# The first mixer's input products of two chunks by a seven-product scheme from the third channel block on, and scaled weights split at their first use

## The chip, the cores and the metric

One Trainium2 chip, one of its cores. The metric is the device time of one execution in microseconds (us). Before the change the median of three timed runs is 1886.26 us (1881.32, 1886.26 and 1886.28).

## What is computed

A decoder trunk of two layers over x of 1 x 2048 x 1024 float32. Layer 0 is a gated short convolution, layer 1 an attention without softmax over 8 heads of 64 whose keys and values come from one shared projection.

```
h = rmsnorm(x, norm_a);  B, C, X, G = split(h @ w_in_a, 4)        # 1024 x 4096
x = x + ((B * conv3(C * X)) * silu(G)) @ w_out_a                  # causal, width 3
k, v = split(rmsnorm(x, norm_kv) @ w_kv, 2)                       # 1024 x 1024
q, g = split(rmsnorm(x, norm_b) @ w_in_b, 2)                      # 1024 x 1024
z = (q @ k.T) / 8, strictly causal
rev = reverse cumulative sum over keys of log_sigmoid(-z)
o = exp(z + rev) @ v
x = x + (o * silu(g)) @ w_out_b
out = rmsnorm(x, norm_f)
```

## The kernel before

Everything is kept transposed (features on the partitions, positions along the free axis, in reverse order) and worked in four chunks of 512 positions, c = 0 to 3. The 1024 features are KD = 8 tiles of 128. Every operand is split into a high part (a cast on ACT, L175) and a low part (a subtraction on DVE, L176, in `split`), and a product is three matmuls per tile: hi x hi, hi x lo, lo x hi. So one gate of one channel block for one chunk (`mm3`, L209) is 8 x 3 = 24 matmuls of 128x512. A gate's raw weights (`wr_*`, 512 KB) come by a DMA that SP issues, are split into a tile `whl_*` of 1 MB, and are stored to DRAM in split form (`sw_*`); whoever needs them again loads that (`load_w`, L184 to L196). There are 4 buffers for split tiles (NWB) and 2 for raw ones (NRAW).

The program starts with `mixer_in((0, 1))`: the input products of chunks 0 and 1 together, so that a weight tile serves both. Its loop runs over the 8 channel blocks cb and in each over the two chunks, and takes the gates C, X, B, G in that order: 8 x 2 x 4 = 64 gates. Gate results lie in three pairs of PSUM banks in turn. Behind the gates ACT and DVE compute the convolution (`cv_*`, L339 and after) and the gating (`sg_*`), and SP stores `y_d[c][cb]`. The norm of chunks 0 and 1 is applied late: the products run on x times the gain, and 1/rms (`rs_c`) multiplies afterwards. While that goes on, a second stream computes the statistics of chunks 2 and 3 (`stats_x`) and runs `fold_gains` (L359 to L372): it multiplies all of w_kv and w_in_b by their norm's gain on DVE (L368), splits them and stores them in DRAM, 32 half tiles of 128x512.

After it `proj_out(0)` (`po_*`, L376) reads y back, splits it and multiplies by w_out_a; `proj_k`, `proj_q` and `proj_v` of chunk 0 follow (12 gates, with four of `proj_g` later), interleaved with `mixer_in((2,))` and the attention of chunk 0; then the other chunks in the same manner, and a tail with the output projection and the last norm.

The program is written as generators that `merge` interleaves by estimated costs. The order of the instructions on each engine is then fixed when the program is built, by a scheduler which simulates the engines. On the chip each engine takes its list in order and waits where an operand isn't ready. A DMA on SP's list that waits for something holds up every DMA behind it.

Of the kernel before, what the change touches and what calls it, by code (L numbers as in the profile page):

```python
# [8 lines left out]
F32 = mybir.dt.float32  # L9
# [5 lines left out]
P = 128  # L15
S = 2048
D = 1024
# [4 lines left out]
NR, NW, NT, NL, NWB, NRAW, NA, NWTS = 5, 8, 4, 5, 4, 2, 16, 2  # L22
# [7 lines left out]
NB = 3  # L30
GRP, GRY, SLACK = 3, 6, 8
# [14 lines left out]
def kernel(  # L46
# [117 lines left out]
    def square_into(acc, src, first, nm, eng=nc.vector, early=False):  # L164
        if first:
            nc.scalar.activation(acc, src, AF.Square)
        else:

            tag = "wth" if early else "t"
            sq = sb.tile([P, CH], F32, name=f"sq_{nm}", tag=tag, bufs=NT if tag == "t" else NWTS)  # L170
            nc.scalar.activation(sq, src, AF.Square)
            eng.tensor_add(acc, acc, sq)
# [5 lines left out]
    def w_tile(nm, kt=KD):  # L178
        return sb.tile([P, 2, kt, P], F32R, name=f"whl_{nm}", tag="whl", bufs=NWB)
# [4 lines left out]
    def load_w(src, key, nm, kt=KD, eng=nc.vector):  # L184

        if key not in split_d:
            wt = w_tile(nm, kt)
            raw = sb.tile([P, kt, P], F32, name=f"wr_{nm}", tag="wraw", bufs=NRAW)
            nc.sync.dma_start(out=raw, in_=src.rearrange("(k p) n -> p k n", p=P))
            split(wt[:, 0], wt[:, 1], raw, eng)  # L190
            split_d[key] = dram.tile([P, 2, kt, P], F32, name=f"sw_{nm}")
            nc.sync.dma_start(out=split_d[key], in_=wt.bitcast(F32))
            return wt
        wt = w_tile(nm, kt)
        nc.sync.dma_start(out=wt.bitcast(F32), in_=split_d[key])
        return wt  # L196
# [6 lines left out]
    def mm3(ps, wts, a, kt=KD):  # L203

        hi, lo = wts[:, 0], wts[:, 1]
        n = 0
        for k in range(kt):
            for w, m in ((hi, 0), (hi, 1), (lo, 0)):
                ins = nc.tensor.matmul(ps, w[:, k, :], a[k][:, m, :], start=n == 0, stop=n == 3 * kt - 1)  # L209
                if fine[1] and len(anchors) > SLACK and n % GRP == 0:  # L210

                    tc.add_manual_dep(ins.ins, anchors[-1 - SLACK].ins.name, PACE, reason="pace")
                n += 1
                if n % fine[0] == 0 and n < 3 * kt:
                    yield MM * fine[0]

    def rest(n):
        return MM * (n - (n - 1) // fine[0] * fine[0])
# [7 lines left out]
    def norm_x_late(c, between=None):  # L226

        hc, xs = [], []
        for k in range(KD):
            if k == 1 and between is not None:  # L230
                between()
            tag, bufs = (("w", NW), ("R", NR) if k < NR else ("ld", NL))[c]
            x = sb.tile([P, CH], F32, name=f"xh_{c}_{k}", tag=tag, bufs=bufs)
            nc.sync.dma_start(out=x, in_=xT[k * P:(k + 1) * P, cols(c)])
            xs.append(x)
            ga = gains["a"][:, k:k + 1]
            hk = act_tile(f"h_{c}", k)
            nc.scalar.activation(hk[:, 0, :], x, AF.Copy, scale=ga)
            nc.vector.scalar_tensor_tensor(out=hk[:, 1, :], in0=x, scalar=ga, in1=hk[:, 0, :].bitcast(F32),
                                           op0=ALU.mult, op1=ALU.subtract)  # L240
            hc.append(hk)
        return hc, xs

    def squares(c, xs):
        acc = sb.tile([P, CH], F32, name=f"acc_h{c}", tag="acc", bufs=2)
        for k, x in enumerate(xs):
            square_into(acc, x, k == 0, f"h{c}{k}", nc.gpsimd, early=True)
        return acc

    def late_rms(c, y):  # L250
        pb = bcast(y, f"h{c}")
        r = sb.tile([P, CH], F32, name=f"rs_{c}", tag="w", bufs=NW)
        nc.scalar.copy(r, pb)
        r2 = sb.tile([P, CH], F32, name=f"rs2_{c}", tag="w", bufs=NW)
        nc.scalar.activation(r2, pb, AF.Square)
        return r, r2

    rx = {}

    def stats_x(c):  # L260

        acc = sb.tile([P, CH], F32, name=f"acc_h{c}", tag="acc", bufs=2)
        for k in range(KD):
            square_into(acc, load_x(c, k, "s"), k == 0, f"h{c}{k}", early=True)
        y = const.tile([P, 4], F32, name=f"rx_{c}")
        rx[c] = rstd(acc, f"h{c}", y)
        yield 1.0
# [14 lines left out]
    late_acc, late = {}, {}  # L282

    def mixer_in(cs):
# [3 lines left out]
        for cb in range(KD):  # L288
            wts = {}
            for c in cs:  # L290
# [5 lines left out]
                def gate(g, i):  # L296
                    if c not in h:
                        if c == 0:
                            load_first = lambda: wts.update({g: load_w(w_src(i), (g, cb), f"{g}{cb}_{cs[0]}")})
                            h[c], late_acc[c] = norm_x_late(c, load_first)  # L300
                        else:
                            h[c], xs = norm_x_late(c)
                            late_acc[c] = rstd(squares(c, xs), f"h{c}")
# [43 lines left out]
                if c in late:  # L347
                    nc.vector.tensor_mul(sg, pG, late[c][0])
                    nc.scalar.activation(sg, sg, AF.Sigmoid)
                    nc.vector.tensor_mul(t, t, late[c][1])  # L350
# [3 lines left out]
                nc.vector.tensor_mul(t, t, pG)  # L354
                nc.sync.dma_start(out=y_d[c][cb], in_=t)
                yield rest(24)


    def fold_gains():  # L359

        for nm, src, gain in (("kv", w_kv, gains["kv"]), ("b", w_in_b[0], gains["b"])):
            for i in range(KD):
                split_d[nm, i] = dram.tile([P, 2, KD, P], F32, name=f"sw_{nm}{i}")
                for j in range(0, KD, 4):
                    hi, lo = (sb.tile([P, 4, P], F32R, name=f"fold{m}_{nm}{i}_{j}", tag="og", bufs=KD) for m in range(2))
                    raw = lo.bitcast(F32)
                    nc.sync.dma_start(out=raw, in_=src[j * P:(j + 4) * P, i * P:(i + 1) * P].rearrange("(k p) n -> p k n", p=P))
                    nc.vector.tensor_mul(raw, raw, gain[:, j:j + 4].unsqueeze(2).to_broadcast([P, 4, P]))  # L368
                    split(hi, lo, raw)
                    for m, t in enumerate((hi, lo)):  # L370
                        nc.sync.dma_start(out=split_d[nm, i][:, m, j:j + 4, :], in_=t.bitcast(F32))
                yield 1.0  # L372
# [3 lines left out]
    def proj_out(c):  # L376

        y = []
        for k in range(KD):
            y.append(act_tile(f"y_{c}", k))  # L380
            t = ld512(f"yr_{c}_{k}")
# [27 lines left out]
    def proj_k(c, kb):  # L409
        wts = load_w(None, ("kv", kb), f"k{c}_{kb}")  # L410
# [9 lines left out]
    def proj_q(c, qb):  # L420
        wts = load_w(None, ("b", qb), f"q{c}_{qb}")
# [7 lines left out]
    def proj_v(c, vb):  # L429
        wts = load_w(None, ("kv", 4 + vb), f"v{c}_{vb}")  # L430
# [12 lines left out]
    def proj_g(c, gb):  # L443
        wts = load_w(None, ("b", 4 + gb), f"gg{c}_{gb}")
# [175 lines left out]
    def out_b_last(c):  # L620
# [3 lines left out]
        for ob in range(KD):  # L624
# [3 lines left out]
            yield from mm3(ps, wts, og, kt=3)  # L628
# [10 lines left out]
        for ob in range(KD):  # L639
            ps = lin(f"pol_{ob}")  # L640
            yield from mm3(ps, wl[ob // 4][:, :, ob % 4:ob % 4 + 1, :], og[3:4], kt=1)
# [88 lines left out]
    run(take(m01, TA / 4))  # L730
    merge((m01, 1.75 * TA), (chain(iter((DLY,)), stats_x(2), stats_x(3), fold_gains()), 18.0 + DLY))
# [47 lines left out]
```

## Time and profile before

| | |
|---|---|
| timed runs | 1881.32 to 1886.28 us, median 1886.26 |
| profiled execution | 1879.31 us, its span 1877.6 us |
| PE, busy share of the span | 94% |
| DVE, ACT, POOL | 67%, 41%, 24% |
| mean granted PE clock | 0.979 |
| DMA | 460.44 MB, 245 GB/s |
| mixer of chunks 0 and 1 | from the start to 369.4 us, where `po` begins |

The span is that of the profiled execution between its first and last instruction; the 1.7 us outside it belong to the launch. PE is TensorE, DVE VectorE, ACT ScalarE, POOL GpSimd, SP the engine that issues most DMAs. Busy shares are means over stages with different limits, so the parts below go by stages.

### The profile page before, as it was taken

The page shows a single profiled execution, that of the slowest core. Times are in us where ns is not written, and L with a number is a line of the kernel's source. Part 1 is how long each engine was busy: PE and PEld are TensorE (multiplying, and loading weights), DVE is VectorE, ACT ScalarE, POOL GpSimd, SP SyncE. Part 2 cuts the span into 40 slices and gives each one's busy share as a digit, 9 for nine tenths or more (in the row PEclk, how much of TensorE's full clock was granted, in tenths as well). Part 3 has the DMA queues.
Part 4 walks back from the last instruction along what each step waited for, and adds up shares of the span by engine and source line. Part 5 has one row for each costly group of instructions (what it writes and reads, how often), then busy time and mean ns, then how long its engine had stood idle before and what let it go on. Part 6 is the DMA issues. An engine that isn't in the chain of part 4 may idle for free.

```text
span 1877.6 us, 24951 instructions
## 1 busy us (share of the span) xinstructions
PE 1771.9 (94%) x8312; PEld 1447.6 (77%) x8312; DVE 1261.9 (67%) x1927; ACT 772.7 (41%) x1497; POOL 450.4 (24%) x822
## 2 busy tenths in 40 slices
PE   7999999999999999999999999999988998988783
PEld 5888888888778878887888888888766886866562
DVE  7876534554243364478785478787858889889984
ACT  6423212231232143345443244454535556556642
POOL 5100000101111032132221122232223214547543
PEclk9999999999999999999999999999999999999896
DMA  9999865697978798867677766566586667778763
GB/s 292 309 324 332 307 195 165 209 328 280 336 250 281 227 330 257 290 207 250 216 253 244 248 195 204 183 215 198 180 300 196 223 194 265 260 238 278 225 196 130
DMA packets 238480, 460.44 MB, mean 245 GB/s; under 512 B 18448, under 2 KB 133136, under 8 KB 213776
## 3 DMA queue, kind: packets, MB, share of 16 engines
q1 hardware_dynamic: 178272, 400.09, 63.0%
q10 hardware_dynamic: 59920, 58.74, 10.9%
q8 instruction: 66, 1.08, 0.2%
q14 instruction: 62, 0.51, 0.1%
q0 software_dynamic: 160, 0.02, 0.1%
HBM read 322.73 MB, written 136.05 MB: 244 GB/s over the span
## 4 chain that ended last, share of the span: by engine, by line
PE 74%; DVE 10%; DMA 7%; issue 4%; ACT 2%; POOL 2%; SPq 0%; ACTq 0%; POOLq 0%; DVEq 0%
PE pX L209 9%; PE pB L209 9%; PE po L209 9%; PE pG L209 9%; PE pC L209 8%; PE wt L526 4%; PE pv L209 4%; PE pk L209 3%; PE pq L209 3%; DVE R L514 3%; PE pg L209 3%; PE av L536 3%; PE av L535 2%; PE z L500 2%; PE z L501 2%
## 5 line engine op out<-in xcount | busy, mean ns | idle before, releaser
L514 DVE TENSOR_TENSOR_SCAN R<-R,R,ones 128x512 f32<-128x512 f32 x192 | 255.0, 1330 | 25.2 <-ACT R L503 24.7
L503 ACT ACTIVATE R<-z 128x512 f32<-128x512 f32 (+1 forms) x320 | 174.0, 544 | 185.0 <-PE z L501 72.7
L176 DVE TENSOR_TENSOR wtl<-wt,wth 128x512 fp32r<-128x512 f32 (+1 forms) x320 | 186.2, 601 | 79.9 <-ACT wth L175 76.8
L175 ACT CAST wth<-wt 128x512 fp32r<-128x512 f32 (+1 forms) x320 | 159.6, 528 | 184.7 <-PE wt L526 150.3
L518 DVE TENSOR_TENSOR w<-w,R 128x512 f32<-128x512 f32 (+1 forms) x320 | 207.7, 658 | 19.6 <-POOL R L511 2.1
L209 PE MATMUL pC<-h,whl_C 128*128 128x512 f32 x768 | 189.8, 396 | 11.0 <-ACT whl_C L175 8.0
L513 POOL COPY R<-R 128x1 f32<-128x1 f32 x192 | 117.4, 613 | 340.9 <-DVE R L514 308.6
L209 PE MATMUL po<-y,whl_o 128*128 128x512 f32 x768 | 189.2, 393 | 2.4 <-DVE x L394 2.0
L209 PE MATMUL pX<-h,whl_X 128*128 128x512 f32 x768 | 186.3, 392 | 1.3 <-DVE cv L354 1.3
L209 PE MATMUL pB<-h,whl_B 128*128 128x512 f32 x768 | 185.9, 392 | 0.0
L209 PE MATMUL pG<-h,whl_G 128*128 128x512 f32 x768 | 185.7, 392 | 0.0
L526 PE MATMUL wt<-ident,w 128*128 128x128 f32 x1088 | 176.8, 278 | 7.5 <-DVE w L518 4.5
L209 PEld LDWEIGHTS pC<-h,whl_C 128*128 128x128 f32 x768 | 143.5, 189 | 44.1 <-ACT whl_C L175 8.0
L505 ACT ACTIVATE w<-z 128x512 f32<-128x512 f32 (+1 forms) x320 | 172.1, 543 | 2.5 <-PE wt L526 2.4
L209 PEld LDWEIGHTS pX<-h,whl_X 128*128 128x128 f32 x768 | 143.5, 188 | 31.5 <-DVE cv L354 1.5
L209 PEld LDWEIGHTS po<-y,whl_o 128*128 128x128 f32 x768 | 142.7, 188 | 32.1 <-DVE x L394 2.2
L209 PEld LDWEIGHTS pB<-h,whl_B 128*128 128x128 f32 x768 | 143.5, 188 | 29.7
L209 PEld LDWEIGHTS pG<-h,whl_G 128*128 128x128 f32 x768 | 143.6, 188 | 29.5
L526 PEld LDWEIGHTS wt<-ident,w 128*128 128x128 f32 x1088 | 137.4, 143 | 36.0 <-DVE w L518 6.9
L536 PE MATMUL av<-wtl,vv 128*128 128x512 f32 (+1 forms) x320 | 127.3, 401 | 27.0 <-DVE wtl L176 26.5
L514 DVE TENSOR_TENSOR_SCAN R<-R,ones 128x512 f32<-128x512 f32 (+3 forms) x128 | 116.4, 915 | 37.0 <-POOL R L509 32.8
L500 PE MATMUL z<-kt,q 128*128 128x512 f32 (+1 forms) x320 | 129.3, 406 | 5.7 <-ACT w L505 2.8
(172 smaller groups left out, 2685.1 us busy)
## 6 DMA issues: line engine op xcount, KB each, us to landing
whl_o<-sw_o SPq DMA_DIRECT2D x24, 1024.0 KB, 5.3
kt<-k_d ACTq DMA_DIRECT2D x80, 256.0 KB, 4.0
vv<-v_d ACTq DMA_DIRECT2D x80, 256.0 KB, 3.7
whl_C<-sw_C SPq DMA_DIRECT2D x16, 1024.0 KB, 5.9
whl_X<-sw_X SPq DMA_DIRECT2D x16, 1024.0 KB, 5.3
whl_B<-sw_B SPq DMA_DIRECT2D x16, 1024.0 KB, 5.8
whl_G<-sw_G SPq DMA_DIRECT2D x16, 1024.0 KB, 5.3
whl_k<-sw_kv SPq DMA_DIRECT2D x16, 1024.0 KB, 7.0
```

The lines of the kernel that those rows point to most:

```text
L175: nc.scalar.copy(hi, src)
L176: eng.tensor_sub(lo, src, hi.bitcast(F32))
L209: ins = nc.tensor.matmul(ps, w[:, k, :], a[k][:, m, :], start=n == 0, stop=n == 3 * kt - 1)
L500: nc.tensor.matmul(ps[:, lom:CH], q2[:, 0, qi * P:(qi + 1) * P], kt[:, lom:CH], start=True, stop=False)
L501: nc.tensor.matmul(ps[:, lom:CH], q2[:, 1, qi * P:(qi + 1) * P], kt[:, lom:CH], start=False, stop=True)
L503: nc.scalar.activation(R[:, lo + 1:CH + 1], ps[:, lo:CH], AF.Sigmoid, scale=-0.125)
L505: nc.scalar.activation(w[:, lo:CH], ps[:, lo:CH], AF.Sigmoid, scale=0.125)
L513: nc.gpsimd.tensor_copy(R[:, 0:1], carry[qi])
L514: nc.vector.tensor_tensor_scan(out=R[:, lo + 1:CH + 1], data0=R[:, lo + 1:CH + 1], data1=ones[:, 0:1].to_broadcast([P, CH - lo]), initial= ...
L518: nc.vector.tensor_mul(w[:, lo:CH], w[:, lo:CH], R[:, lo:CH])
L526: nc.tensor.transpose(wt[:, qi * P:(qi + 1) * P], ws[qi][:, kb * P:(kb + 1) * P], ident)
L536: ins = nc.tensor.matmul(av[:, 0:n], vs, wl[:, 0:n], start=False, stop=final)
```

## The change

Five edits go together.

1. **Seven products for eight.** `mixer_in((0, 1))` runs as before for channel blocks 0 and 1 (NPL = 2). From block 2 on `mixer_fast` takes the gates in pairs, (C, X) and (B, G): 12 units. A unit is two gates by two chunks by two halves of the features, which are eight half products of 4 x 3 = 12 matmuls. The scheme of Strassen in Winograd's form does it with seven: a11 by b11, s1 by t1, s2 by t2, s4 by b22, a12 by b21, s3 by t3, a22 by t4, where a are weight half tiles, b the halves of x in the two chunks, and s and t sums and differences of them. Three banks collect them; ACT copies four partial sums out (`keep`), DVE adds.
2. **Operands for it.** During block 1 `fast_operands` scales x of both chunks by gain and 1/rms (16 DVE operations), POOL forms 16 differences, and 28 tiles are split (a cast and a subtraction each). For each unit `fast_weights` loads four raw half tiles of 256 KB, splits eight tiles, stores four.
3. **`fold_gains` is gone.** w_kv and w_in_b are scaled and split where first used (`gain=` in `load_w`): 12 gates in the projections of chunk 0, and four in `proj_gate(2)` much later.
4. **Half tiles.** A weight tile holds 4 of the 8 feature tiles: 8 buffers of 512 KB for 4 of 1 MB, 4 raw buffers of 256 KB for 2 of 512 KB. Each weight DMA becomes two.
5. **Small ones.** The late gating uses Silu and drops a DVE product; the last block of y for chunk 0 stays on the chip; buffers move (x of chunk 1 lies in the buffers `og`, `ld`, `vv` and `ot`), and the two `merge` lines get other numbers.

```diff
-NR, NW, NT, NL, NWB, NRAW, NA, NWTS = 5, 8, 4, 5, 4, 2, 16, 2
+NR, NW, NT, NL, NWB, NRAW, NA, NWTS = 5, 8, 4, 5, 8, 4, 16, 2
+NPL = 2
+Q = 4
...
+        for j in range(0, kt, Q):
+            wt = w_tile(f"{nm}_{j}")
+            if first:
+                raw = sb.tile([P, Q, P], F32, name=f"wr_{nm}_{j}", tag="wraw", bufs=NRAW)
+                nc.sync.dma_start(out=raw, in_=src[j * P:(j + Q) * P, :].rearrange("(k p) n -> p k n", p=P))
+                if gain is not None:
+                    nc.vector.tensor_mul(raw, raw, gain[:, j:j + Q].unsqueeze(2).to_broadcast([P, Q, P]))
+                split(wt[:, 0], wt[:, 1], raw, eng)
+                nc.sync.dma_start(out=split_d[key][:, :, j:j + Q, :], in_=wt.bitcast(F32))
+            else:
+                nc.sync.dma_start(out=wt.bitcast(F32), in_=split_d[key][:, :, j:j + Q, :])
...
-        for cb in range(KD):
+        for cb in range(KD if len(cs) == 1 else NPL):
+            if cb == NPL - 1 and len(cs) > 1:
+                fast_operands()
...
-    def fold_gains():
...
+    def fast_weights(n, cb, gs):
+        if n % 2 == 0:
+            raws = [sb.tile([P, Q, P], F32, name=f"fr_{nm}_{i}", tag="wraw", bufs=NRAW) for i in range(4)]
+        else:
+            pair = sb.tile([P, 2, Q, P], F32, name=f"fr_{nm}", tag="hl", bufs=1)
+            raws = [pair[:, 0], pair[:, 1]] + [sb.tile([P, Q, P], F32, name=f"fr_{nm}_{i}", tag="ot", bufs=2) for i in range(2)]
...
+            if key == "a22":
+                nc.vector.tensor_add(a22, a21, a22)
+                sp("s1", a22)
+                nc.gpsimd.tensor_sub(a21, a11, a21)
+                nc.vector.tensor_sub(a11, a22, a11)
+                sp("s2", a11)
+        nc.gpsimd.tensor_sub(a12, a12, a11)
+        sp("s4", a12)
+        sp("s3", a21)
...
+    def mixer_fast():
+            for k in range(Q):
+                for i, m in ((0, 0), (0, 1), (1, 0)):
+                    beat[:] = [nc.tensor.matmul(bank, w[:, i, k, :], ops[b][k][m], start=start and n == 0,
...
+            yield product(a, w["a11"], "b11", True, False)
+            c0 = keep(f"f1_{nm}", a)
+            yield product(d, w["s1"], "t1", True, False)
+            p5 = keep(f"f5_{nm}", d)
+            if not final:
+                ws[n + 1] = fast_weights(n + 1, *units[n + 1])
+            if prev:
+                yield last_product(n - 1)
+            yield product(a, w["s2"], "t2", False, False)
+            c1 = keep(f"f2_{nm}", a)
+            yield product(d, w["s4"], "b22", False, True)
+            nc.vector.tensor_add(c1, c1, d)
+            if not final:
+                yield product(c, w["a12"], "b21", True, True)
+                nc.vector.tensor_add(c0, c0, c)
+            yield product(a, w["s3"], "t3", False, False)
...
-        wts = load_w(None, ("kv", kb), f"k{c}_{kb}")
+        wts = load_kv(kb, f"k{c}_{kb}")
...
-    run(take(m01, TA / 4))
-    merge((m01, 1.75 * TA), (chain(iter((DLY,)), stats_x(2), stats_x(3), fold_gains()), 18.0 + DLY))
+    run(take(m01, TA / 2))
+    merge((m01, 1.3 * TA), (chain(iter((DLY,)), stats_x(2), stats_x(3)), 2.0 + DLY))
```

How it moves the instructions shows at three places. The first is DVE at the end of channel block 1, which in the changed program comes right before the first unit with B and G (`B2`). `op_t4_2` and `op_t4_3` are operands made from x of chunk 1 (`xh_1_6`, `xh_1_7`), `cv_1_1` is the plain gating of block 1, `f1_C2` a sum of the unit before, `fr_B2_0` and `fr_B2_1` are raw weights and `whl_*_B2` their split tiles.

```order
L177 TENSOR_TENSOR op_t4_2_1_1154<-xh_1_6_555,op_t4_2_0_1153 128x512
L374 TENSOR_TENSOR cv_1_1_1059<-cv_1_1_1059,sg_1_1_1089 128x512
L177 TENSOR_TENSOR op_t4_3_1_1158<-xh_1_7_560,op_t4_3_0_1157 128x512
L560 TENSOR_TENSOR f1_C2_1218<-f1_C2_1218,fc_C2_1205 128x512
L177 TENSOR_TENSOR whl_a21_B2_1246<-fr_B2_0_1235,whl_a21_B2_1246 128x512
L177 TENSOR_TENSOR whl_a22_B2_1251<-fr_B2_1_1236,whl_a22_B2_1251 128x512
L465 TENSOR_TENSOR fr_B2_1_1236<-fr_B2_0_1235,fr_B2_1_1236 128x512
L177 TENSOR_TENSOR whl_s1_B2_1256<-fr_B2_1_1236,whl_s1_B2_1256 128x512
```

Before, the weights of a gate needed one such subtraction; now the tile s1 needs two loads, two casts, an addition, a cast and a subtraction. Counted from the first product of `fast_operands` with the 1/rms of chunk 1, the third of these rows is the 70th on DVE (14 products with a scalar, 56 additions, subtractions and products of two tiles) and the last the 75th.

The second place is SP at the same time. `fr_B2_0` and `fr_B2_1` take the two buffers `ot` in which `xh_1_6` and `xh_1_7` lie; `y_d_1_1` is the store of `cv_1_1`.

```order
L463 DMA sw_B2_1244<-whl_a11_B2_1241 256x1x512
L458 DMA fr_B2_0_1235<-in_w_in_a_dram 128x4x128
L377 DMA y_d_1_1_96<-cv_1_1_1059 128x512
L458 DMA fr_B2_1_1236<-in_w_in_a_dram 128x4x128
```

Both loads can be issued only when DVE has read `xh_1_6` and `xh_1_7` for the rows `op_t4_2` and `op_t4_3` above. On PE the first product that needs them, s1 by t1 of unit B2, stands behind seven products: a11, s1, a12, s2, s4 and s3 of unit C2 and a11 of unit B2.

The third place is SP in the projections of chunk 0. Before, the split weights of a gate came in one load each (`whl_*`, from `sw_*`):

```order
L195 DMA whl_k0_1_3913<-sw_kv1_1426 128x2048
L195 DMA whl_q0_1_3947<-sw_b1_2264 128x2048
L195 DMA whl_v0_1_3978<-sw_kv5_1834 128x2048
```

Now raw halves (`wr_*`) are loaded, and the halves split before them (`whl_*`) stored, by turns:

```order
L201 DMA sw_k0_1_4151<-whl_k0_1_0_4152 256x1x512
L197 DMA wr_v0_1_0_4244<-in_w_kv_dram 128x4x128
L201 DMA sw_k0_1_4151<-whl_k0_1_4_4159 256x1x512
L197 DMA wr_v0_1_4_4251<-in_w_kv_dram 128x4x128
L201 DMA sw_q0_1_4198<-whl_q0_1_0_4199 256x1x512
L197 DMA wr_v0_2_0_4295<-in_w_kv_dram 128x4x128
```

So a raw load stands behind a store which waits for the split of an earlier gate; before, a load waited only for a free buffer.

In the whole program PE has 144 matmuls fewer, DVE 140 operations more, ACT 153 more and POOL 40 more, and SP issues 166 DMAs more.

219 lines of the change are left out of this document (174 added, 45 removed).

## The prediction

> **What bounds the kernel now.** I read the page first: the busy shares, the slices, and the chain that ended last, by engine.
>
> ```profile
> PE 1771.9 (94%) x8312; PEld 1447.6 (77%) x8312; DVE 1261.9 (67%) x1927; ACT 772.7 (41%) x1497; POOL 450.4 (24%) x822
> PE   7999999999999999999999999999988998988783
> DVE  7876534554243364478785478787858889889984
> PE 74%; DVE 10%; DMA 7%; issue 4%; ACT 2%; POOL 2%; SPq 0%; ACTq 0%; POOLq 0%; DVEq 0%
> ```
>
> PE is busy for 94% of the span and carries 74% of the last chain. A slice is 47 us, so the mixer of chunks 0 and 1 is the first eight, and in seven of them PE shows a 9. What a change there is worth is read from that stage, so the next view is the busy time by stretches (PE, PEld, DVE, ACT, POOL busy us, granted PE clock, DMA share, GB/s).
>
> ```profile
> 0.00:10.00 10.00, 2.01 (x4) 1.13 (x5) 3.03 (x5) 4.84 (x6) 5.97 (x13) 1.00 0.91 169
> 10.00:20.00 10.00, 7.27 (x22) 3.77 (x21) 7.70 (x7) 9.04 (x15) 6.43 (x5) 1.00 1.10 314
> 40.00:50.00 10.00, 8.77 (x43) 7.24 (x42) 9.93 (x23) 5.78 (x11) 2.99 (x2) 1.00 0.77 220
> 60.00:100.00 40.00, 40.00 (x178) 33.13 (x177) 28.05 (x45) 14.18 (x24) 1.42 (x5) 1.00 0.86 298
> 100.00:200.00 100.00, 100.00 (x451) 83.10 (x450) 68.15 (x117) 29.41 (x43) 4.25 (x9) 1.00 0.97 333
> 200.00:300.00 100.00, 100.00 (x443) 82.90 (x442) 45.98 (x61) 20.83 (x28) 3.76 (x11) 1.00 0.68 220
> 300.00:369.00 69.00, 69.00 (x306) 57.21 (x305) 31.74 (x41) 17.78 (x24) 5.83 (x8) 1.00 0.58 184
> 470.00:520.00 50.00, 45.15 (x203) 36.30 (x202) 15.91 (x23) 11.10 (x26) 8.09 (x25) 0.98 0.90 322
> 1200.00:1400.00 200.00, 194.05 (x951) 158.66 (x949) 160.97 (x242) 100.33 (x205) 57.65 (x104) 0.98 0.64 216
> ```
>
> From 60 to 369 us PE has no idle time and a clock of 1.00. The chain of waits, read over that stretch, shows the same as pieces (start, us, engine, tile, line, matmuls):
>
> ```profile
> 62.38 1.37 PE pC L209 x6
> ...
> 68.32 5.44 PE pX L209 x24
> ...
> 106.40 5.44 PE pC L209 x24
> ...
> 369.43 5.45 PE po L209 x24
> ```
>
> A gate is 5.44 us for 24 matmuls, 226.7 ns each, and gate follows gate until `po` starts. The gate at 62.38 begins channel block 1, that at 106.40 block 2. In this stage matmuls alone set the time, so one that is left out is worth its 0.2267 us, as long as nothing else becomes late.
>
> **Matmuls removed.** A unit has 8 half products of 12 matmuls before and 7 after. 12 units x 12 = 144 matmuls x 0.2267 us = **-32.6 us**. A unit then lasts 84 x 0.2267 = 19.04 us.
>
> **What a unit asks of the others.** These rows give the prices, the first two from a stretch in which DVE works back to back (five operations each), the last from the groups.
>
> ```profile
> 375.51 3.38 DVE L274 SCALAR_TENSOR_TENSOR xn<-xn,g_a,prb_hb 128x512 f32<-128x512 f32 x5
> 378.81 3.09 DVE L176 TENSOR_TENSOR h<-xn,h 128x512 fp32r<-128x512 f32 x5
> L175 ACT CAST fold_kv<-fold_kv 128x512 fp32r<-128x512 f32 x16 | 9.9, 621 | 32.8 <-DVE fold_kv L368 32.8
> L172 POOL TENSOR_TENSOR acc_h<-acc_h,sq_h 128x512 f32<-128x512 f32 x14 | 21.2, 1515 | 8.9 <-ACT sq_h L171 8.4
> ```
>
> DVE: some 18 operations (8 splits, 2 sums of weights, 3 of products, 5 of convolution and gating) at 0.62 to 0.68 us, 11 to 12 us. ACT: 8 casts, 4 copies, 2 others at 0.62, 8.7 us. POOL: two subtractions at 1.52, 3.0 us. DMA: 4 x 256 KB in and 4 x 512 KB out, 3 MB in 19.04 us, 165 GB/s, where the stretch from 100 to 200 us carried 333. All is under 19.04, and a bank that ACT must copy before PE adds to it again (f2 before s3 by t3) has two products, 5.4 us, for a copy of 0.6. I cost the units' extra work at nothing: PE's own products hide it. If that cover is gone, it is a rival below.
>
> **Entering the new scheme.** Here DVE gets a pile. It can begin with the operands when 1/rms of chunk 1 is there; before, that was first used at
>
> ```profile
> 67.20 0.69 DVE L331 TENSOR_TENSOR p<-p,rs 128x512 f32<-128x512 f32 x1 [1.91 <-ACT rs L255]
> ```
>
> so 4.8 us after block 1 began (call that t0). The order has 70 operations from there to the low part of `op_t4_3`: 14 x 0.68 + 56 x 0.62 = 44 us, done at t0+49. Only then SP can load `fr_B2_1`. Nearest row for that load, the 256 KB raw halves from 60 to 350 us:
>
> ```profile
> fold_b<-in_w_in_b_dram SPq DMA_DIRECT2D x16, 256.0 KB, 6.1
> ```
>
> 6.1 us, then a cast, two subtractions, an addition, a cast and a subtraction, some 3.8 us: s1 of B2 is ready at t0+59. PE asks for it after block 1 (8 x 5.44 = 43.5) and seven products (19.0), at t0+62.5. That is 3.5 us to spare, if DVE runs at its usual speed. But POOL has 18 subtractions in just this time, 18 x 1.52 = 27 us, and the trace shows what the two do to each other (first DVE with POOL quiet, then both):
>
> ```profile
> 9.08 0.75 DVE L239 SCALAR_TENSOR_TENSOR h<-xh,g_a,h 128x512 fp32r<-128x512 f32 x1
> ```
>
> ```profile
> 29.09 2.89 DVE L239 SCALAR_TENSOR_TENSOR h<-xh,g_a,h 128x512 fp32r<-128x512 f32 x2
> ```
>
> ```profile
> 26.07 8.75 POOL L172 TENSOR_TENSOR acc_h<-acc_h,sq_h 128x512 f32<-128x512 f32 x5 [0.27 <-ACT sq_h L171]
> ```
>
> The same DVE operation takes 1.45 us instead of 0.75, a POOL operation 1.75. During 27 to 31 us of POOL work DVE loses 48% of its pace, 13 to 15 us; less the 3.5 to spare, PE waits 9.5 to 11.5. Some of the DVE operations read PSUM or meet POOL waiting for its own operands, so I take **+8 us**, with 0 and 14 as ends.
>
> The Trainium skill has a rule for this place ("SBUF — State Buffer", section "SBUF: two separate sides"): GpSimd and a VectorE operation with two SBUF inputs share a port pair, and whichever starts first holds it for its whole instruction while the other blocks fully. The rows agree that they hinder each other; whether DVE then loses each POOL operation's whole length is the rival "POOL first" below. By the rule the term would be about +23 and the sum some 15 us higher.
>
> **Leaving it.** Before, `po` follows the last gate with no gap. After, DVE must first finish `sg_7_1` (a Silu, then a product: 1.3 us after the last matmul), in whose wake stand the broadcast's operands for chunk 2, two other splits and the low parts of `y_0`. PE has two matmuls in between. 0.6 (Silu) + 0.62 + some 2.5 for the rest before `y_0_0`: **+3 us**, ends 0 and 6.
>
> **Start.** PE's first wait is
>
> ```profile
> PE pC L209 <- ACT whl_C L175: 8.0, 1, 8.0
> ```
>
> The first weights now come in halves of 256 KB, and a cast takes 0.62 us where a whole tile took two such. But in the second stretch of the table PE waited again 2.7 us, for x. **-1.5 us**, ends -4 and +2.
>
> **First uses in the projections of chunk 0.** The time of `fold_gains` lay beside full PE and was worth nothing; its work now stands where PE is full but the DMA is too. From 400 to 550 us:
>
> ```profile
> DMA packets 14392, 42.67 MB, mean 284 GB/s; under 512 B 1315, under 2 KB 6408, under 8 KB 11309
> q1 hardware_dynamic: 11546, 38.54, 71.9%
> q10 hardware_dynamic: 2837, 4.01, 9.5%
> ...
> xn_d<-xn SPq DMA_DIRECT2D x8, 512.0 KB, 10.1
> whl_k<-sw_kv SPq DMA_DIRECT2D x4, 1024.0 KB, 8.1
> ...
> x<-in_xT_dram SPq DMA_DIRECT2D x8, 256.0 KB, 7.5
> ```
>
> The queues are busy for 81%; 12 gates x 0.5 MB more (0.5 raw in and 1 out for 1 in) is 6 MB, which makes 93%. DVE's 12 x 2 x 2 operations more, 30 us, fit: in the table it is busy 15.91 of 50 there. SP's list puts raw loads behind stores, and with four raw buffers a round of two gates is load, product, cast, subtraction: 7.5 + 0.62 + 0.62 + 0.62 = 9.4 us by the 256 KB row, 12 by the 10.1 of the other, for 10.88 us of PE. Over six rounds that is 0 to 7 us: **+3 us**, ends -3 and +15.
>
> The Trainium skill ("DMA: Bandwidth & Descriptors", section "Bandwidth") wants transfers of 1 MiB or more and gives 138 GB/s at 64 KB and 341 at 1 MB; halving every weight DMA goes against it. In the rows above a quarter of the bytes lands in nearly the same time, 7.5 for 8.1 us, so the landing is mostly not size. As an estimate from that page the 0.5 MB of raw weights of a gate take between 1.5 us (at 341) and 3.8 us (at 138); were the difference exposed at all 12 gates, it would cost 27 us, and the sum would be some 24 us higher.
>
> **The rest.** Four first uses in `proj_gate(2)`: 16 DVE operations, 10 us, in the stretch 1200 to 1400, where DVE is 80% busy and PE 97%: **+1**, ends 0 and 3. The later order is reshuffled on every engine; with nothing in the trace to give it a sign I take 0, ends -8 and +8.
>
> **Sum**, against the profiled execution's 1879.31 us (span 1877.6 and 1.7 around it): -32.6 + 8 + 3 - 1.5 + 3 + 1 = -19.1, so **1860 us**. The median of the timed runs, 1886.26, lies 7 us above that execution, so a median after may lie as far above the sum.
>
> **Rivals.**
>
> *All of the gain.* POOL hardly meets DVE at the entry, and nothing is late: the term of 8 goes, and with it 3 at most of the others, 1849 to 1852. For it: the 3.5 us to spare. Against: the slowed rows. 20%.
>
> *POOL first.* DVE loses the whole 27 us at the entry: 27 - 3.5 = 23 for 8, 1875. Against: at 29.09 two DVE operations took 2.89 us in all, where waiting for a whole POOL operation each would take 2 x (0.75 + 1.52) = 4.5. 10%.
>
> *The units don't close.* The saving is there, but each unit waits for its sums or weights. From 1.6 us a unit on (12 x 1.6 = 19.2) the sum is back at 1879. For it: DVE's 12 us and POOL's 3 of 19 are strung in one chain for each unit. Against: 4.5 us or more to spare. 8%.
>
> *First uses in single file (slower).* On SP a raw load stands behind a store that waits for a split two gates back. If loads and stores go strictly by turns, a round of two gates takes two chains, 2 x 9.4 = 18.8 us, for 10.88 of PE: 6 x 7.9 = 47 us for 3, 1904. It outweighs the gain from a round of 10.88 + 22 / 6 = 14.5 us on. For it: the DMA at 93% and the order on SP. Against: four raw buffers, and attention work of chunk 0 between the gates. 12%.
>
> That the change doesn't do what it says is excluded for the matmuls: they are counted in the order.
>
> **Chances.** Forecast 50% (1852 to 1870), all of the gain 20%, POOL first 10%, units 8%, single file 12%. A measurement of this kernel tells some 0.3%, 5.6 us, from no change. Faster by more holds the forecast, the full gain, half of POOL first and a quarter of the units: 0.77. Slower by more: single file, mostly, 0.11. Within: the other half, the units' rest and the middle of single file, 0.12. The range leaves out the far end of single file and a little of the full gain with a lucky later order: 1844 to 1885.
>
> **What would show it.** PE in the mixer: 84 matmuls every 19.0 us from block 2 on, with idle time only at s1 of B2 (wait for `whl_s1_B2`, 8 us), and `po` starting near 369.4 - 32.6 + 8 - 1.5 = 343 us. DVE's subtractions of 0.62 us should show 1.4 us and more while POOL subtracts. After `po`: a wait of 3 us for `y_0` or the broadcast. Between there and 520: waits of PE for `whl_k0`, `whl_q0`, `whl_v0` of a few us in all. It would be wrong if PE waits inside the units, or if those weights are late by more than 2 us at each gate.

## The result, and the profile after

The changed kernel takes 1908.44 us (median of four runs, 1904.85 to 1914.92), the kernel before beside it 1884.47. The ratio is 1.0133 with a 95% interval of 1.0101 to 1.0165: it is slower, by some 24 us. The forecast was 1860, 19 us faster than the profiled execution before. The profiled execution after took 1908.73 us, its span is 1907.0.

The page of the kernel after, busy shares, the slices of PE and of its granted clock, and the last chain by engine:

```profile
span 1907.0 us, 25384 instructions
PE 1767.4 (93%) x8168; PEld 1430.4 (75%) x8168; DVE 1346.3 (71%) x2067; ACT 836.4 (44%) x1650; POOL 498.9 (26%) x862
PE   7989999899899989999999999999889988988784
PEclk9989999999899989999999999999999998989986
PE 65%; DVE 14%; DMA 9%; issue 6%; ACT 2%; POOL 2%; SPq 1%; ACTq 0%; POOLq 0%; DVEq 0%
```

The 144 matmuls are gone (8312 to 8168), but PE's busy time fell by 4.5 us only, not by 32.6. Two things stand against it. PE is idle 1907.0 - 1767.4 = 139.6 us, before 105.7: 33.9 more. And its matmuls run at a lower clock: the mean granted clock is 0.965, before 0.979, which is 66.7 us lost for 39.4 (share below 1 times span), 27 more. 33.9 + 27.3 - 32.6 = 28.6, and the span grew by 29.4. So there is one account: the matmuls were saved, and they were taken back twice, once by new waits of PE and once by the lower clock. That the clock falls behind a wait can be seen at the entry below.

Where the waits are, five marks tell, the starts of PE's matmuls of the same tiles in both profiles (timeline):

| PE starts | before | after | difference |
|---|---|---|---|
| block 2 (first C, or first seven-product unit) | 106.23 | 107.74 | +1.5 |
| `po` of chunk 0 | 369.26 | 356.34 | -12.9 |
| `pk` of chunk 0 | 469.68 | 464.06 | -5.6 |
| `pk` of chunk 1 | 692.95 | 704.17 | +11.2 |
| `pol`, the last output product | 1847.91 | 1877.67 | +29.8 |

Each stage loses something. The first loss is the entry into the new scheme. Timeline of PE in the kernel after (start, length, engine, line, operation; in brackets the idle time before it and what ended it):

```profile
107.74 2.95 PE L483 MATMUL fa_C<-op_b,whl_a_C 128*128 128x512 f32 x12
110.53 2.94 PE L483 MATMUL fd_C<-op_t,whl_s_C 128*128 128x512 f32 x12
113.31 1.79 PE L483 MATMUL fc_C<-op_b,whl_a_C 128*128 128x512 f32 x7
117.42 1.97 PE L483 MATMUL fc_C<-op_b,whl_a_C 128*128 128x512 f32 x5 [2.32 <-DVE op_b L177]
122.68 1.19 PE L483 MATMUL fa_B<-op_b,whl_a_B 128*128 128x512 f32 x2 [3.29 <-DVE sg L369]
124.24 4.91 PE L483 MATMUL fa_C<-op_t,whl_s_C 128*128 128x512 f32 x12 [0.37 <-ACT f_C L493]
```

PE waits for the low part of an operand (b21). Then it waits for a product on DVE:

```profile
121.86 0.68 DVE L369 TENSOR_TENSOR sg<-pG,rs 128x512 f32<-128x512 f32 x1
```

It belongs to the last plain gate: it reads the gate's result `pG` out of PSUM, and its bank is one of the two that `fa_C` and `fa_B` take in turn (tag `lin`), so `fa_B` can't begin before. The twelve matmuls behind it take 4.91 us and not 2.7. The stretches beside it (columns as in the prediction):

```profile
110.00:120.00 10.00, 7.07 (x27) 4.77 (x26) 9.97 (x11) 6.95 (x13) 7.20 (x5) 0.91 0.37 115
120.00:130.00 10.00, 6.95 (x19) 5.10 (x20) 7.94 (x12) 2.11 (x4) 0.78 (x1) 0.58 0.42 128
```

The clock column reads 0.91 and 0.58: the share below 1 is 0.9 + 4.2 us, so the clock stood at half for some 10 us. Finer stretches show when it fell, after the first of the two waits (115.1 to 117.4 us) and before the second:

```profile
114.00:118.00 4.00, 1.68 (x7) 1.05 (x6) 4.00 (x4) 3.77 (x8) 3.37 (x3) 1.00 0.38 112
118.00:119.40 1.40, 1.39 (x4) 0.57 (x2) 1.40 (x1) 0.77 (x2) 1.40 (x2) 0.54 0.02 7
```

The product s1 by t1 of the next unit (`fd_B`) starts at 137.50, 29.76 us after the first product; the seven products ahead of it need 19.04. The entry costs 10.7 us.

### The profile page after: what moved, and what is told of

It reads as the page before. It is cut to its first block, busy times and chain, and to the rows that moved or that the text cites. A ratio compares the mean times of both kernels' runs of the same rounds, so it can differ in the third digit from the quotient of the medians.

```text
span 1907.0 us, 25384 instructions
## 1 busy us (share of the span) xinstructions
PE 1767.4 (93%) x8168; PEld 1430.4 (75%) x8168; DVE 1346.3 (71%) x2067; ACT 836.4 (44%) x1650; POOL 498.9 (26%) x862
## 4 chain that ended last, share of the span: by engine, by line
PE 65%; DVE 14%; DMA 9%; issue 6%; ACT 2%; POOL 2%; SPq 1%; ACTq 0%; POOLq 0%; DVEq 0%
PE po L217 7%; PE pX L217 5%; PE pC L217 5%; PE pG L217 4%; PE pv L217 4%; PE wt L736 4%; PE pB L217 4%; PE pk L217 3%; DVE R L724 3%; PE pg L217 3%; PE pq L217 3%; PE fa_B L483 3%; PE fa_C L483 3%; PE av L746 2%; PE av L745 2%
## 5 line engine op out<-in xcount | busy, mean ns | idle before, releaser
L723 POOL COPY R<-R 128x1 f32<-128x1 f32 x192 | 105.2, 549 | 370.7 <-DVE R L724 333.8
L745 PE MATMUL av<-wth,vv 128*128 128x512 f32 (+1 forms) x320 | 124.0, 388 | 21.1 <-ACT wth L176 20.3
L710 PE MATMUL z<-kt,q 128*128 128x512 f32 (+1 forms) x320 | 130.8, 411 | 13.2 <-ACT w L715 10.8
L217 PE MATMUL pC<-h,whl_C 128*128 128x512 f32 x480 | 123.9, 401 | 11.7 <-ACT whl_C L176 6.8
L719 POOL TENSOR_SCALAR_AFFINE_SELECT R<-R 128x128 f32<-128x128 f32 x128 | 60.4, 472 | 268.6 <-ACT R L713 256.8
L711 PE MATMUL z<-kt,q 128*128 128x512 f32 (+1 forms) x320 | 121.4, 382 | 0.0
L217 PE MATMUL pG<-h,whl_G 128*128 128x512 f32 x480 | 119.5, 394 | 1.1 <-DVE whl_G L177 1.1
L217 PE MATMUL pX<-h,whl_X 128*128 128x512 f32 x480 | 118.9, 392 | 0.8 <-DVE whl_X L177 0.5
L217 PE MATMUL pB<-h,whl_B 128*128 128x512 f32 x480 | 118.4, 392 | 0.0
L217 PEld LDWEIGHTS pC<-h,whl_C 128*128 128x128 f32 x480 | 90.3, 191 | 34.5 <-ACT whl_C L176 6.8
```

What stands on the lines that cost most here:

```text
L217: ins = nc.tensor.matmul(ps, wts[k // Q][:, w, k % Q, :], a[k][:, m, :], start=n == 0, stop=n == 3 * kt - 1)
L710: nc.tensor.matmul(ps[:, lom:CH], q2[:, 0, qi * P:(qi + 1) * P], kt[:, lom:CH], start=True, stop=False)
L711: nc.tensor.matmul(ps[:, lom:CH], q2[:, 1, qi * P:(qi + 1) * P], kt[:, lom:CH], start=False, stop=True)
L745: nc.tensor.matmul(av[:, 0:n], vs, wh[:, 0:n], start=first, stop=False)
```

## The experiments

Each ran beside the kernel before, on the same chip. "Net" is the difference of the medians. Marks are those of the table above, in each run's own profile. The tables below call the kernels, in the order of the sections, half_tiles, first_use, eight_products, whole_reloads, fold_back, subs_on_vector, two_dma, other_order, vector_whole, vector_whole_bcast, vector_all and vector_all_fold.

### Half tiles alone

```diff
-        wt = w_tile(nm, kt)
-        nc.sync.dma_start(out=wt.bitcast(F32), in_=split_d[key])
...
+        for j in range(0, kt, Q):
+            wt = w_tile(f"{nm}_{j}")
...
+            else:
+                nc.sync.dma_start(out=wt.bitcast(F32), in_=split_d[key][:, :, j:j + Q, :])
```

> The kernel before with the half tiles alone (8 buffers of 512 KB, 4 raw ones of 256 KB, two DMAs for each weight tile). Theory 'halves' (more DMAs in the same queues delay the attention's loads and the weights after the mixer, and that is the loss behind the mixer): 15 to 40 us slower than before, 1900 to 1925. Theory 'first uses' (scaling and splitting w_kv and w_in_b in the projections is the loss): within 5 us of before. Theory 'order' (any rearrangement of the later instructions costs or gains some us by chance): up to 10 us either way.

1894.70 for 1881.83, ratio 1.0059 (1.0036 to 1.0081): net +12.9, a little under the 15 to 40 of "halves". Up to `pk` of chunk 1 it is only 1.4 us behind the kernel before, at `pk` of chunk 3 1.9 and at `pol` 10.8: most of the loss sits in the last quarter of the program.

### First uses alone

```diff
+            if gain is not None:
+                nc.vector.tensor_mul(raw, raw, gain.unsqueeze(2).to_broadcast([P, kt, P]))
...
-    merge((m01, 1.75 * TA), (chain(iter((DLY,)), stats_x(2), stats_x(3), fold_gains()), 18.0 + DLY))
+    merge((m01, 1.75 * TA), (chain(iter((DLY,)), stats_x(2), stats_x(3)), 2.0 + DLY))
```

> The kernel before without fold_gains, with the scaling and the splits of w_kv and w_in_b at their first use, in whole tiles. Theory 'first uses': 15 to 40 us slower than before, most of it lost in the projections of chunk 0 (before: pk to po of chunk 1, 130 us). Theory 'halves': within 5 us of before. Theory 'order': up to 10 us either way.

1889.71 for 1881.83, ratio 1.0038 (1.0023 to 1.0054): net +7.9, less than expected. The place is as expected: from `pk` of chunk 0 to `pk` of chunk 1 it loses 14.3 us, and later gains 5.9 back. Part of both numbers is work that changed places: 30 matmuls of the attention, at most 6.8 us (30 x 0.2267), stand ahead of `pk` of chunk 1 here and behind it before. With the 12.9 of the half tiles that makes 20.8 us, so both theories hold a part.

### Eight products with all other edits

```diff
-NPL = 2
+NPL = KD
...
-        if len(cs) > 1:
-            yield from mixer_fast()
```

> The changed kernel with eight products in all channel blocks (no seven-product scheme, no operands for it); half tiles, first uses, buffers and merge lines as changed. If halves and first uses together are the loss behind the mixer (42 us by the two profiles), this is 30 to 42 us slower than before, 1915 to 1925, and the seven products are still worth some 10 to 15 us. If the loss comes with the seven products (through the order or the buffers they leave behind), this is within 10 us of before.

1901.19 for 1881.83, ratio 1.0104 (1.0075 to 1.0133): net +19.4, between the two cases. That is about the 20.8 of half tiles and first uses alone, so the small edits and the `merge` lines, which this kernel has too, need not cost anything. The seven products as they were built take nothing away: the changed kernel's net is +24.0. That they add to the loss isn't shown, since the two intervals overlap. In the profile the changed kernel is 14.6 us ahead of this one at `po` of chunk 0, and 1.3 ahead at `pk` of chunk 1.

### Whole tiles for the reloads

```diff
+        else:
+            nc.sync.dma_start(out=wt.bitcast(F32), in_=split_d[key])
+        return [wt[:, :, j:j + Q] for j in range(0, kt, Q)]
```

> The changed kernel with weight tiles whole again (4 of 1 MB; a reload is one DMA of 1 MB; raw loads and first stores stay halves; the seven-product units use the halves of a tile). Theory 'halves': 15 to 35 us faster than the changed kernel, 1873 to 1893. Theory 'first uses': within 5 us of it. Theory 'order': up to 10 us either way.

1896.53 for 1881.83, ratio 1.0077 (1.0050 to 1.0104): net +14.7 for +24.0. Fewer microseconds than "halves" expected, because the mixer now loses: `po` of chunk 0 begins 8.4 us later than in the changed kernel. At the entry PE waits 6.3 and 2.0 us for `whl_a_C`, the a12 of the first unit, whose cast stands on ACT behind those of the operands, and its low part on DVE behind their slowed subtractions; behind the entry it waits 3.8 us for ACT's copies (`f_B`), and ACT's casts of weights wait up to 7.2 us for products of PE. That both come from half tiles which share a whole one is argued, not shown. From `pk` of chunk 1 to `pol` it loses nothing against before (-3.4).

### The fold back beside the mixer

```diff
-    merge((m01, 1.3 * TA), (chain(iter((DLY,)), stats_x(2), stats_x(3)), 2.0 + DLY))
+    merge((m01, 1.3 * TA), (chain(iter((DLY,)), stats_x(2), stats_x(3), fold_gains()), 18.0 + DLY))
```

> The changed kernel with fold_gains back beside the mixer of chunks 0 and 1 (in the seven-product units DVE has 7 us of 19 to spare), so that the projections load split weights as before; seven products and half tiles stay. Theory 'first uses cost some 10 us in the projections of chunk 0': 8 to 14 us faster than the changed kernel, 1894 to 1900, and po of chunk 1 begins no later than before plus what the mixer left. Rival: whatever is gained early is lost again by a bound that is the same for all variants (DMA): within 4 us of the changed kernel.

1908.61 for 1882.40, ratio 1.0131 (1.0104 to 1.0158): net +26.2, the changed kernel's loss, but not by the rival's bound. In the projections the loss is gone (`pk` to `pk`: 3.6 us, for 16.8). In the mixer it lost more than that: `po` of chunk 0 begins 21.8 us later than in the changed kernel. The theory of the first uses stands. The prediction's "worth nothing" for the time of `fold_gains` held beside eight products (without it, first_use reached `po` no earlier than the kernel before), and not beside seven.

### The operands' differences on DVE

```diff
-            nc.gpsimd.tensor_sub(x0[k], x1[k], x0[k])
+            nc.vector.tensor_sub(x0[k], x1[k], x0[k])
```

(and so the twelve others of `fast_operands` and `fast_rest`)

> The changed kernel with the 16 differences of the operands computed by DVE and not by POOL (those of the units' weights stay on POOL). Theory 'contention' (POOL slows DVE at the entry): DVE gets 16 x 0.62 = 10 us more work and loses 13 to 15 us less; the entry, 12 us of PE's time now, shrinks by 3 to 6 us. Theory 'pile' (what counts is the number of operations behind the release of the operand slots): the entry stays or grows by up to 10 us.

1886.77 for 1882.40, ratio 1.0027 (1.0011 to 1.0043): net +4.4, so 20 us better than the changed kernel by an edit that moves 16 small operations. The two kernels side by side, DVE's column the third (busy us, operations in brackets), POOL's the fifth; the changed kernel:

```profile
70.00:80.00 10.00, 10.00 (x46) 8.29 (x45) 10.00 (x15) 3.86 (x7) 7.01 (x4) 1.00 0.00 0
80.00:90.00 10.00, 10.00 (x46) 8.29 (x45) 10.00 (x8) 2.47 (x4) 10.00 (x7) 1.00 0.00 0
90.00:100.00 10.00, 10.00 (x45) 8.28 (x45) 10.00 (x12) 4.46 (x9) 7.21 (x6) 1.00 0.15 55
```

with the differences on DVE:

```profile
70.00:80.00 10.00, 10.00 (x46) 8.29 (x45) 10.00 (x17) 4.32 (x8) 2.98 (x1) 1.00 0.00 1
80.00:90.00 10.00, 10.00 (x46) 8.29 (x45) 10.00 (x18) 3.33 (x7) 2.51 (x2) 1.00 0.00 0
90.00:100.00 10.00, 10.00 (x46) 8.29 (x45) 10.00 (x17) 5.34 (x11) 4.13 (x1) 1.00 0.36 134
110.00:120.00 10.00, 9.80 (x44) 7.67 (x42) 8.76 (x16) 4.60 (x10) 5.95 (x1) 1.00 0.22 77
120.00:130.00 10.00, 9.21 (x41) 7.28 (x40) 6.50 (x11) 3.29 (x7) 0.00 (x0) 1.00 0.67 204
```

DVE is "busy" all the time in both, but from 80 to 90 us it finishes 8 operations beside 7 of POOL, and 18 without. Operation by operation in the changed kernel, DVE and then POOL:

```profile
81.11 1.78 DVE L177 TENSOR_TENSOR op_t<-xh,op_t 128x512 fp32r<-128x512 f32 x1
82.81 1.77 DVE L352 TENSOR_TENSOR p<-p,rs 128x512 f32<-128x512 f32 x1
84.51 1.78 DVE L177 TENSOR_TENSOR op_t<-xh,op_t 128x512 fp32r<-128x512 f32 x1
86.21 0.67 DVE L364 TENSOR_TENSOR cv<-cv,pB 128x512 f32<-128x512 f32 x1
```

```profile
80.60 1.74 POOL L428 TENSOR_TENSOR xh<-xh,xh 128x512 f32<-128x512 f32 x1
82.30 1.74 POOL L419 TENSOR_TENSOR xh<-xh,xh 128x512 f32<-128x512 f32 x1
```

They go in step, one DVE operation and one POOL operation every 1.70 us; only the one that reads PSUM (`pB`) takes its 0.67. The entry shrinks: `po` begins 8.6 us earlier, PE's clock stays at 1.00. "Contention" is shown; its size at the entry was 9, above the 3 to 6 expected. The end gains 22 us in the profile and not 8.6: the others fall in the stretches behind `pk` (7.4 and 6.1), in which nothing was edited. The wait of 9.4 us at 698 us (below) is gone there; why is open.

### Two DMAs and nothing else

```diff
-        nc.sync.dma_start(out=wt.bitcast(F32), in_=split_d[key])
+        for j in range(0, kt, 4):
+            nc.sync.dma_start(out=wt[:, :, j:j + 4, :].bitcast(F32), in_=split_d[key][:, :, j:j + 4, :])
```

> The kernel before with nothing changed but that a reload of a split weight tile comes in two DMAs into the halves of one whole tile. Half tiles alone cost 13 us. Theory 'number of DMAs' (shared queues fill up with twice the transfers): 8 to 13 us slower than before. Theory 'order' (the small tiles make the scheduler place the later work otherwise): within 4 us of before.

1890.93 for 1882.40, ratio 1.0050 (1.0034 to 1.0065): net +8.5, as "number of DMAs" has it. Two thirds of the half tiles' 12.9. The order of the later work also moves with it, so the time alone doesn't separate the two.

### Another order and nothing else

```diff
-F0, F1, F2, F3, F4 = 0.4, 0.5, 0.65, 0.4, 0.6
+F0, F1, F2, F3, F4 = 0.4, 0.5, 0.65, 0.4, 0.55
```

> The kernel before with the constant F4 at 0.55 for 0.6: no work changes, only the order of the later attention and mixer instructions (about one in seven from the second half of the gates on stands elsewhere). Theory 'order': 4 to 12 us away from before. If the later loss comes from the DMAs or the first uses, it is within 3 us of before.

1879.59 for 1882.40, ratio 0.9976 (0.9960 to 0.9992): net -2.8. That is within the 3 us, against "order". A different order costs or gains a few microseconds; on the way to the end its gates lie between 7.8 us ahead and 3.6 behind. That is one sample. But behind `pk` of chunk 1 this kernel lost 2.1 us, and the six with two DMAs for a reload 6.7 to 18.5 (table below).

### Whole tiles, differences on DVE, and another order of the splits

```diff
-                nc.vector.tensor_add(a22, a21, a22)
-                sp("s1", a22)
-                nc.gpsimd.tensor_sub(a21, a11, a21)
...
+        nc.vector.tensor_add(a21, a21, a22)
+        sp("s1", a21)
...
+        first("a22", a22, gs[1], Q)
+        nc.gpsimd.tensor_sub(a22, a22, a11)
+        sp("s3", a22)
```

(and the edits of "Whole tiles for the reloads" and "The operands' differences on DVE")

> The changed kernel with three things together: the operands' 16 differences on DVE, whole weight tiles with one DMA for a reload, and in the seven-product units another order of the splits (s3 from a22 - s2, the halves paired as a11 with s1, a21 with a12, s2 with s4, a22 with s3), so that no tile is held by a late product. Theories: the entry loses little (as with the differences on DVE, about 2 us), the units lose nothing, and the reloads in one DMA give back the 8 to 13 us that two DMAs cost: 1872 to 1880, 2 to 10 us faster than before. If two DMAs are not what the later stages lose by, it stays near 1887.

1881.66 for 1881.41, ratio 0.9999 (0.9985 to 1.0013): the loss is gone, without a gain, and 2 us short of the 1872 to 1880 expected. The later stages lose nothing (-1.8 from `pk` of chunk 1 to `pol`), but the stretch of the first uses 19.3 us. Three edits go together here, so the gain isn't divided among them.

### The broadcast for chunk 2 earlier

```diff
+    def broadcast(c):
+        early[c] = bcast(rx[c], f"hb{c}")
+        yield 1.0
```

> As vector_whole, and the broadcast of 1/rms for chunk 2 is made during the units and not at the start of the output product. Theory 'leaving' (PE waits there for the broadcast's operands on DVE, two waits of 1.9 us, and its clock falls): 4 to 7 us faster than vector_whole. Rival: the wait moves to the low parts of y, and it is within 2 us.

1873.86 for 1881.41, ratio 0.9948 (0.9931 to 0.9966): 7.8 better than vector_whole, but not where it was expected. `po` to `pk` of chunk 0 loses 7.9 us here and 7.4 there: PE now waits 4.3 and 2.2 us for `y`, so the rival is right about the leaving. What differs is again between `pk` and `pk` (12.8 for 19.3); why is open.

### All differences on DVE

```diff
-        nc.gpsimd.tensor_sub(a12, a12, a11)
+        nc.vector.tensor_sub(a12, a12, a11)
...
-        nc.gpsimd.tensor_sub(a22, a22, a11)
+        nc.vector.tensor_sub(a22, a22, a11)
```

> As vector_whole, with the units' two differences of weights on DVE as well, so that POOL subtracts nothing in the mixer. Theory 'contention in the units too' (two POOL operations slow DVE in each unit): 2 to 5 us faster than vector_whole. Rival: the units have DVE time to spare and it is within 1.5 us.

1865.88 for 1881.41, ratio 0.9919 (0.9888 to 0.9950). This version beats both kernels, by 15.5 and some 40 us. At `po` of chunk 0 it is 4.0 us ahead of vector_whole, at `pk` of chunk 0 7.2, at `pk` of chunk 1 14.7; the expected 2 to 5 fit the first number, the rest is once more the place behind.

### The same with the fold back

> As vector_all, with fold_gains back beside the mixer, so that the projections load split weights. Theory 'first uses' (every run with first uses lost 9 to 19 us between pk of chunk 0 and pk of chunk 1 against before, every run without them 0 to 4): it loses no more than 4 us there. In the mixer two theories: if the units were disturbed by fold_gains only because POOL slowed DVE, the mixer ends no later than in vector_all and the whole is 6 to 12 us faster, 1854 to 1860; if ACT's copies wait behind the casts of the folded weights whatever POOL does, po begins 10 to 25 us later and the whole is the same or slower than vector_all.

1878.41 for 1882.74, ratio 0.9991 (0.9972 to 1.0010): 12.5 us worse than vector_all by the medians. The first half of the expectation held (from `pk` to `pk` it gains 0.9 on the kernel before, vector_all loses 11.8), and of the two theories on the mixer the second: `po` begins 13.5 us later though POOL subtracts nothing (busy 14.18 of 240 us from 110 to 350). PE waits there for copies of ACT (3.4 and 1.6 us) and for weights (4.0 and 1.4).

## Why the prediction was wrong

The marks give each step its measured size. A mark isn't the same place in every order: in the kernels with first uses 22 to 30 matmuls of the attention changed from behind `pk` of chunk 1 to ahead of it, at most 5.0 us in the changed kernel (22 x 0.2267). So of the differences below, the one from `pk` to `pk` is up to 5 us too large, and the one behind it as much too small.

**The saving: right.** -32.6 us of matmuls. Behind the entry the units nearly keep their 19.04 us: from 137.50 to the last product's end at 354.11 stand 924 matmuls, 209.4 us, in 216.6; 1.6 of the rest are two small sums (`pst_h`) that were there before. "The units don't close" is out. So is "single file" as worked out: the loop of two chains would have cost 47 us, and the stretch lost 16.8. That its sum, 1904, lies near the measured 1908.44 is chance.

**The start: wrong in sign, small.** Forecast -1.5, measured +1.5 at block 2.

**The entry: mechanism right, too small, and its waits in another place.** Forecast 8, from 1.45 us for a slowed DVE operation. Measured 10.7, which lies within the 9.5 to 11.5 that the prediction worked out before it took a discount. The row of 1.45 was a mean of two; in the same view before, the operations beside it had already taken what the changed kernel shows:

```profile
26.81 1.75 DVE L239 SCALAR_TENSOR_TENSOR h<-xh,g_a,h 128x512 fp32r<-128x512 f32 x1
31.97 1.70 DVE L239 SCALAR_TENSOR_TENSOR h<-xh,g_a,h 128x512 fp32r<-128x512 f32 x1
```

Beside back-to-back subtractions of POOL a DVE operation takes 1.70 to 1.78. The waits fell on b21 and on the bank that `sg` frees, and not on s1, since the pile delays everything in DVE's list. But s1 of B2 was the limit that came last: its low part was ready at 137.6 us (136.27 + 1.32), just when PE reached `fd_B`. The rule of the Trainium skill ("SBUF — State Buffer", section "SBUF: two separate sides"), by which one blocks the other for a whole instruction, is closer to the 1.70 than the prediction's discount was; by the trace the two then alternate.

**Leaving: 3 forecast, 9.5 measured** (2.2 us from the last product's end to `po`, and 7.3 from there to `pk` of chunk 0). The waits are those named, the broadcast's operands (3.8 us) and DVE:

```profile
PE prb_hb L161 <- DVE dg_hb L160: 3.8, 2, 1.9
PE pC L217 <- DVE cv L364: 1.6, 1, 1.6
PE po L217 <- DVE x L604: 1.2, 1, 1.2
```

and the clock column reads 0.63 from 356 to 360 us and 0.95 from 360 to 400, which is 1.5 + 2.0 us more.

**First uses: 3 forecast, 16.8 measured from `pk` to `pk`.** The DMA's share was forecast right: 93%, and from 400 to 550 us it is 0.93, before 0.82. What was wrong is where it would show. The prediction looked for waits on the split weights, and no wait of PE in the stretch is for one. PE is idle for 10.6 us more than before, at the attention's matmuls for the most part, and loses 6.8 us more by the clock. From 470 to 560 us, before and then after:

```profile
470.00:560.00 90.00, 85.15 (x386) 69.61 (x385) 31.84 (x51) 23.71 (x54) 14.21 (x42) 0.96 0.85 292
```

```profile
470.00:560.00 90.00, 81.12 (x364) 65.56 (x363) 57.71 (x93) 34.72 (x77) 16.83 (x48) 0.94 0.98 325
```

The DMA's share goes from 0.85 to 0.98, and PE does 22 matmuls less. The longest wait comes later: at 698 us PE waits 9.4 us for one cast, though ACT had stood idle; ACT's list in the kernel after:

```profile
685.57 0.73 ACT L359 ACTIVATE cv<-p,cw 128x512 f32<-128x512 f32 x1 [6.05 <-DMA x<-in_xT_dram]
687.51 0.45 ACTq L695 DMA_DIRECT2D q<-q_d  x1
692.66 0.33 ACTq L702 DMA_DIRECT2D kt<-k_d  x1
693.03 0.58 ACT L753 COPY ot<-av 64x512 f32<-64x512 f32 x1 [6.73 <-DMA x<-in_xT_dram]
696.92 0.56 ACTq L704 DMA_DIRECT2D vv<-v_d  x1
697.88 0.97 ACT L176 CAST wth<-wt 128x512 fp32r<-128x512 f32 x2 [4.27 <-DMA x<-in_xT_dram]
```

```profile
698.52 0.79 PE L745 MATMUL av<-wth,vv 128*128 128x512 f32 x1 [9.42 <-ACT wth L176]
```

ACT issues the attention's loads (`q`, `kt`, `vv`), and an issue that must wait for an earlier transfer, here SP's load of x, holds up the casts behind it. Why it must wait can be read from the trace's semaphores: the program lets all DMAs of SP and ACT report their landing on the same eight, in turn, and an issue waits until the last DMA on its semaphore has landed. The load of `kt` at 692.66 follows the landing of SP's load of x, issued at 682.35, by 0.02 us, and `vv` at 696.92 follows another by 0.02. In none of the 14 kernels, before and after among them, are more than eight of these under way at once. The runs show that the stretch loses 9 to 19 us in each of the eight kernels with first uses, and 4 or less in those without (half_tiles 0.4, two_dma 2.9, fold_back 3.6, vector_all_fold and other_order below 0). Less the work that changed places, that is still 4 to 14.

**The rest: 1 forecast with the order at 0, 18.5 measured from `pk` of chunk 1 to `pol`.** This is the step that failed most clearly: two DMAs for each reload were given no term of their own, and the order, with ends of -8 and +8, didn't cover them. PE is idle there for 9.9 us more than before and loses 11.6 us more by the clock. From `pk` of chunk 1 to `pol`:

| reload in | kernels | loss |
|---|---|---|
| two DMAs | changed, half_tiles, two_dma, eight_products, fold_back, subs_on_vector | 18.5, 9.4, 6.7, 9.9, 12.8, 12.4 |
| one DMA | first_use, whole_reloads, vector_whole, vector_whole_bcast, vector_all, vector_all_fold, other_order | -5.9, -3.4, -1.8, -1.1, -6.5, 4.8, 2.1 |

The prediction argued that a quarter of the bytes lands in nearly the same time, 7.5 for 8.1 us. That is just the price: of the eight places, a load of half the bytes takes one for nearly as long, before and then after:

```profile
whl_o<-sw_o SPq DMA_DIRECT2D x24, 1024.0 KB, 5.3
whl_o<-sw_o SPq DMA_DIRECT2D x48, 512.0 KB, 5.1
```

In this stretch all eight are taken for 13.4 us before and 38.4 in two_dma; over the kernels it is 23 to 38 us with two DMAs and 13 to 26 with one. The rule of the Trainium skill that it weighed ("DMA: Bandwidth & Descriptors", section "Bandwidth", transfers of 1 MiB or more) points the right way, and two_dma gives the size for this kernel, 8.5 us. The table ties the loss to the edit in all six kernels that have it. By which waits PE then loses the time is argued from ACT's list above, not shown, and a part of the changed order isn't excluded.

**What no step had: the clock.** Each wait was priced by its length. 27 of the 61 us that were lost in all went by the granted clock. The Trainium skill ("TensorE: Matmul & The Clock Gate", section "Part 1: The HAM clock gate") has PE at half its clock after an idle window of some 3.4 us, until it has been busy for as long. The trace agrees in kind and not in length: at the entry the clock fell after a single wait of 2.32 us, and with the second, of 3.29, it stood at half for some 10 us.

Open: why the medians of vector_whole and vector_all differ by 15.8 us when their mixers differ by 4. The place is the stretch around 690 us, where one cast of ACT waits 10.0 us behind a store of y in vector_whole, and PE 5.6 us for it; in vector_all it waits 2.9 behind a load of x, and PE 0.5. Whether that is order or chance of arrival was not tried.

## What to carry to other kernels

When PE is full, work taken from it is worth its time only if nothing that makes room for it touches the lists that PE waits for later: here smaller tiles and moved loads cost 19 us, in stages that have nothing to do with the saving. Count the DMAs as well as the bytes where only so many can be under way. Don't use POOL to relieve DVE when DVE's operations read two tiles in SBUF; on DVE the differences cost 0.6 us each, on POOL they cost DVE 1.1. And price a wait of PE with the clock behind it: at the entry 5.6 us of waiting went with 5.1 us more.

## What the runs showed of the hardware

DVE and POOL, both on two SBUF operands of 128x512 float32, go in step at 1.70 us for one of each (0.60 and 1.3 alone), while a DVE operation with one operand in PSUM keeps its 0.67. "Busy" of 10.00 in 10 us can hold 8 operations or 18, so the count in the bracket has to be read with the time. And an engine's DMA issues stand in its list like computation: ACT stood 6 us and more behind a transfer of SP's, and PE 9.4 behind ACT. And a wait of 2.32 us was enough for PE's granted clock to fall to 0.50, where it stayed for some 10 us, a second wait among them.
